# GpSimd scales the next stage's rows, and the first layer's row loads are tied to the current projection product

## The chip, the cores and the metric

The kernel runs on one core of a Trainium2 chip. The metric is the device time of one execution in microseconds (us). Three timed runs of the kernel before took 2790.7, 2800.73 and 2800.74 us; the median is 2800.73 us. Each engine works through its own list of instructions in order. Engines wait for one another, and for transfers, by semaphores. The engines are named TensorE (PE, with PEld for its weight loads), VectorE (DVE), ScalarE (ACT), GpSimd (POOL) and SyncE (SP), which here only issues DMAs.

## The reference

Two layers work on a sequence of 2048 rows of 1024 numbers, in float32. Each layer normalises every row, projects it, runs two groups of four heads, projects back and adds the result to its input. A last normalisation closes the trunk.

```python
def hybrid_layer(x, norm_w, w_in, ...):
    h = rmsnorm(x, norm_w)
    proj = jnp.einsum('bsd,de->bse', h, w_in)
    mq, mk, mv, mi, mf, mz, aq, ak, av, az = jnp.split(proj, idx, axis=-1)
    ...   # convolution and SiLU on mq, mk; mLSTM over chunks; per-head norm, skip, gate -> ym
    ...   # rotary on aq, ak; softmax1 - lam*softmax2 over earlier chunks; per-head norm, gate -> ya
    y = jnp.einsum('bse,ed->bsd', jnp.concatenate([ym, ya], -1), w_out)
    return x + y

def rmsnorm(x, w):
    y = x * lax.rsqrt(jnp.mean(x * x, axis=-1, keepdims=True) + EPS)
    return y * w
```

The change concerns the first line, `rmsnorm(x, norm_w)`: the sum of squares of each row, and the product of the row with its scale factor.

## The kernel before

**Stages and units.** The 2048 rows are cut into four blocks of 512 (T). A stage is one block in one layer, so there are eight stages; stage s of layer 0 is followed by stage s + 1 on the next block. A stage has four units, one per head of both groups. In a unit TensorE makes the head's projection products (512 rows, the eight 128-column pieces of the input), its attention scores, the products of the weights with the values, and the mLSTM products. The two output projections of a stage are worked off in the stage's last unit and the next stage's second.

**Precision.** Most products are made of split numbers: an operand is stored as a rounded high half and the rest as a low half, and three products are added. A weight tile is therefore loaded (`wr`, L191, SyncE), rounded (`wh`, L193, ScalarE) and subtracted (`wl`, L195, GpSimd). Each of the three has three buffers.

**Preparing a stage's input.** This is what the change touches. `prep_x` (L223) finds the scale factors of the next stage's rows. In layer 1 it reads sums of squares that the output projection of layer 0 left behind. In layer 0, for stages 1 to 3, `row_scale` (L199) loads each of the four 128-row pieces in two halves of 256 KB (L204, eight loads into the four buffers of tile x), ScalarE squares and sums each half (L205), VectorE adds the two sums and makes the mean (L210, L211), GpSimd raises it to the power -1/2 (L212). This call stands at the start of unit 2 (L1080). `prep_t` (L249) then fetches the rows again in four quarters of 256 columns (L258, two loads each, the same four buffers), scales them in place (L272, four instructions of 128x256 per quarter, 16 per stage), transposes them on TensorE (L109), and splits the result into `hth` (L278, ScalarE) and `htl` (L280, VectorE). The first two quarters are fetched early, ahead of the last unit's output projection; a later quarter is fetched when the buffers of an earlier one are free. Stage 0 has its own way (`prep_first`, L231) and isn't touched. So L272 runs 7 x 16 = 112 times.

**The value products of a stage's first head** are evicted by ScalarE (L344, L346) and VectorE (L345), and with them the gate values (gt, L348, VectorE). Only then is their accumulator free for TensorE.

**Rotary work of the next head.** `post_b` (L440) makes the rotated q and k: two VectorE products, four on GpSimd (L448 to L451), then two tiles ab, whose high halves ScalarE rounds (L456) and whose low halves GpSimd subtracts (L457). Sixteen small DMAs (L460, L461) copy pieces of ab into the q and kc tiles from which TensorE makes the next unit's scores.

**What sets the order.** A planner gives every piece of work a time and a stream. TensorE's instructions are tied together: each follows the last of its stream, and a projection product (stream P) also follows all side work (scores A, weights times values V, mLSTM M) that is planned 15 us or more ahead of it. The other engines are ordered by the scheduler of the language, which takes an instruction when its operands and buffers are free in its own model. `after(r, name)` (L87) adds an order without a wait: the scheduler places r behind the named instruction. `last_pe["P"]` is the name of the latest projection product at that point of the program.

Of the kernel before, what the change touches and what calls it, by code (L numbers as in the profile page):

```python
# [16 lines left out]
ALU = mybir.AluOpType  # L17
AX = mybir.AxisListType

P = 128  # L20
S = 2048
D = 1024
T = 512
# [29 lines left out]
def trunk_kernel(ctx, tc, x, w_ch, w_v0, w_v, w_o, nw, cw, cb, gb, mnw, msk, anw, lam,  # L53
                 fnw, rope, out, n_layers=NL, n_t=NT):
    nc = tc.nc
    V, A, G, PE, SY = nc.vector, nc.scalar, nc.gpsimd, nc.tensor, nc.sync
# [11 lines left out]
    def st(shape, tag, dt=F32, name=None):  # L68
        return sb.tile(shape, dt, tag=tag, name=name or tag, bufs=BUFS[tag])

    def sm(cols, name):
        return sb.tile([P, cols], F32, tag="s_" + name, name=name, bufs={"mx": 2, "zc": 2, "nm": 2, "s12": 4}.get(name, 1))

    def pst(tag, shape):
        return psm.tile(shape, F32, tag=tag, name=tag, bufs=PB[tag])

    def f32(ap):
        return ap.bitcast(F32)
# [3 lines left out]
    last_pe = {}  # L82
# [4 lines left out]
    def after(r, name):  # L87
        tc.add_manual_dep(r.ins, name, nosync, reason="TensorE order")
# [19 lines left out]
    def tr(o, i, n=P):  # L108
        pin(PE.transpose(o, i, ident[:n, :n]))  # L109
# [75 lines left out]
    def xin(l, t):  # L185
        return x[t * T:(t + 1) * T, :] if l == 0 else xo[l - 1][t]
# [12 lines left out]
    def row_scale(src, tb, tag):  # L199

        sq = sm(2, "xsq")
        for hf in range(2):
            xt = st([P, T], tag)
            SY.dma_start(xt, src[tb * P:(tb + 1) * P, hf * T:(hf + 1) * T])  # L204
            A.activation(xt, xt, AF.Square, accum_out=sq[:, hf:hf + 1])  # L205
        return row_rms(sq)

    def row_rms(sq):
        rs = sb.tile([P, 1], F32, tag="s_xrs", name="xrs", bufs=8)
        V.tensor_tensor(rs, sq[:, 0:1], sq[:, 1:2], op=ALU.add)  # L210
        V.tensor_scalar(out=rs, in0=rs, scalar1=1.0 / D, scalar2=EPS, op0=ALU.mult, op1=ALU.add)  # L211
        G.tensor_tensor(rs, rs, mhalf[:, 0:1], op=ALU.pow)  # L212
        return rs[:, 0:1]
# [9 lines left out]
    def prep_x(l, t):  # L223
        if l > 0:
            return row_scales(sqs[l - 1, t])
        return [row_scale(xin(l, t), tb, "x") for tb in range(4)]
# [22 lines left out]
    def prep_t(l, t, rs, H, rows=None):  # L249
        pr = par[l]  # L250
        src = xin(l, t)
        qs = {}

        def fetch(q):

            qs[q] = [st([P, 2, 256], "x") for _ in range(2)]
            for i, xt in enumerate(qs[q]):
                SY.dma_start(xt, src[2 * i * P:2 * (i + 1) * P, q * 256:(q + 1) * 256].rearrange("(b p) c -> p b c", p=P))  # L258

        def task(dc):  # L260
            def f():
                if dc == 0:
                    H["rope"] = sb.tile([P, 2, T], F32, tag="rope", name="rope", bufs=1)
                    SY.dma_start(H["rope"], rope[t])
                q, j = divmod(dc, 2)
                if rows:
                    xs = [r_[dc // 4][:, (dc % 4) * P:(dc % 4 + 1) * P] for r_ in rows]
                else:
                    if j == 0:
                        for tb in range(4):  # L270
                            xb = qs[q][tb // 2][:, tb % 2]
                            V.tensor_scalar(out=xb, in0=xb, scalar1=rs()[tb], scalar2=None, op0=ALU.mult)  # L272
                    xs = [qs[q][tb // 2][:, tb % 2, j * P:(j + 1) * P] for tb in range(4)]
                ps = pst("mm", [P, T])
                for tb in range(4):
                    tr(ps[:, tb * P:(tb + 1) * P], xs[tb])
                h = st([P, T], "hth", F32R)
                A.activation(h, ps, AF.Copy, scale=pr["nw"][:, dc:dc + 1])  # L278
                lo = st([P, T], "htl", F32R)
                r_ = V.scalar_tensor_tensor(out=lo, in0=ps, scalar=pr["nw"][:, dc:dc + 1], in1=f32(h),  # L280
                                            op0=ALU.mult, op1=ALU.subtract)
                if rows and dc == 7:
                    first["r"] = r_.ins.name
                H["hh"].append(h)
                H["hl"].append(lo)
                if not rows and j == 1 and q < 2:
                    fetch(q + 2)
            return f

        H["fetch"] = lambda: (fetch(0), fetch(1))  # L290
        return [(0.44, task(dc)) for dc in range(8)]
# [966 lines left out]
```

## Time and profile before

| | |
|---|---|
| median of three runs | 2800.73 us |
| profiled execution | 2792.97 us |
| its span, first to last instruction | 2791.3 us |
| TensorE busy | 2656.9 us, 95% |
| VectorE busy | 1796.1 us, 64% |
| ScalarE busy | 1688.5 us, 60% |
| GpSimd busy | 1439.6 us, 52% |
| mean granted TensorE clock | 0.988 |

Busy is the time in which an engine works on an instruction. Idle time of TensorE is what can be won or lost directly; idle time of the others matters only where TensorE waits for them. A row of waits gives the engine and line that waited, the one that released it, the total, the number and the longest. A row of the timeline gives the start and the length in us, the engine, the line, the operation, the tiles, how many instructions were merged, and in brackets how long the engine stood idle before it and what ended that. The mean granted clock is below 1 where TensorE ran at 1.2 GHz instead of 2.4.

### The profile page before, as it was taken

The page shows a single profiled execution, that of the slowest core. Times are in us where ns is not written, and L with a number is a line of the kernel's source. Part 1 is how long each engine was busy: PE and PEld are TensorE (multiplying, and loading weights), DVE is VectorE, ACT ScalarE, POOL GpSimd, SP SyncE. Part 2 cuts the span into 40 slices and gives each one's busy share as a digit, 9 for nine tenths or more (in the row PEclk, how much of TensorE's full clock was granted, in tenths as well). Part 3 has the DMA queues.
Part 4 walks back from the last instruction along what each step waited for, and adds up shares of the span by engine and source line. Part 5 has one row for each costly group of instructions (what it writes and reads, how often), then busy time and mean ns, then how long its engine had stood idle before and what let it go on. Part 6 is the DMA issues. An engine that isn't in the chain of part 4 may idle for free. (4 is left out here: it accounts for less than half of the span.)

```text
span 2791.3 us, 49265 instructions
## 1 busy us (share of the span) xinstructions
PE 2656.9 (95%) x16692; PEld 2359.0 (85%) x16692; DVE 1796.1 (64%) x4746; ACT 1688.5 (60%) x4541; POOL 1439.6 (52%) x1182
## 2 busy tenths in 40 slices
PE   7999999999999999999999999999999999999997
PEld 6898898888888888888889888978888888887887
DVE  5546565665757767567755465666667676676776
ACT  5655566666656656565556555656566665665665
POOL 5564656545455354344446656555554554445425
PEclk9999999999999999999999999999999999999999
DMA  6645555464644644344556465654557445455333
GB/s 211 173 133 159 178 163 157 135 194 140 191 141 124 189 129 140 117 115 130 162 144 182 142 184 156 196 182 136 177 145 223 145 133 178 118 181 149 100 104 121
DMA packets 249788, 431.01 MB, mean 154 GB/s; under 512 B 30400, under 2 KB 106688, under 8 KB 249536
## 3 DMA queue, kind: packets, MB, share of 16 engines
q1 hardware_dynamic: 249536, 427.87, 51.4%
q8 instruction: 132, 2.16, 0.3%
q14 instruction: 120, 0.98, 0.1%
HBM read 314.38 MB, written 63.05 MB: 135 GB/s over the span
## 5 line engine op out<-in xcount | busy, mean ns | idle before, releaser
L195 POOL TENSOR_TENSOR wl<-wr,wh 128x512 fp32r<-128x512 f32 (+1 forms) x684 | 910.5, 1337 | 1030.7 <-PE mm L106 418.4
L193 ACT ACTIVATE wh<-wr 128x512 fp32r<-128x512 f32 (+1 forms) x684 | 429.1, 629 | 402.6 <-PE mm L106 185.4
L106 PE MATMUL mm<-hth,wh 128*128 128x512 f32 x1536 | 620.1, 404 | 0.0
L106 PE MATMUL mm<-htl,wh 128*128 128x512 f32 x1536 | 611.0, 398 | 0.0
L740 DVE TENSOR_SCALAR_CACHE_REDUCE p<-sc 128x512 f32<-128x512 f32 (+3 forms) x640 | 384.2, 605 | 140.0 <-PE sc L106 113.6
L684 ACT ACTIVATE p<-p,nm 128x512 f32<-128x512 f32 (+3 forms) x640 | 413.9, 649 | 95.8 <-DVE nm L680 87.8
L106 PE MATMUL mm<-hth,wl 128*128 128x512 f32 x1536 | 438.0, 399 | 0.0
L106 PEld LDWEIGHTS mm<-hth,wh 128*128 128x128 f32 x1536 | 291.2, 190 | 59.3 <-ACT vaug L346 0.9
L106 PEld LDWEIGHTS mm<-htl,wh 128*128 128x128 f32 x1536 | 291.3, 190 | 57.2
L106 PEld LDWEIGHTS mm<-hth,wl 128*128 128x128 f32 x1536 | 283.8, 189 | 60.2
L807 DVE TENSOR_TENSOR atl<-tpa,ath 128x512 fp32r<-128x512 f32 x288 | 197.2, 685 | 144.0 <-ACT ath L806 143.0
L704 DVE SCALAR_TENSOR_TENSOR p<-p,s 128x512 f32<-128x512 f32 (+2 forms) x320 | 280.7, 888 | 1.7
L106 PE MATMUL mm<-wh,hth 128*128 128x256 f32 (+1 forms) x1024 | 264.9, 289 | 10.9 <-DVE gt L348 10.5
L106 PE MATMUL mm<-wh,htl 128*128 128x256 f32 (+1 forms) x1024 | 262.0, 286 | 0.0
L806 ACT ACTIVATE ath<-tpa 128x512 fp32r<-128x512 f32 x288 | 170.2, 591 | 148.1 <-PE tpa L109 142.5
L106 PE MATMUL sc<-kp,q 128*128 128x512 f32 x768 | 244.7, 406 | 9.3 <-DVE p L740 9.2
L106 PEld LDWEIGHTS mm<-wh,hth 128*128 128x128 f32 x1024 | 196.1, 191 | 15.8 <-issue 11.5
L106 PEld LDWEIGHTS mm<-wh,htl 128*128 128x128 f32 x1024 | 196.4, 192 | 2.9
L109 PE MATMUL tpa<-ident,p 128*128 128x128 f32 x1088 | 184.4, 274 | 13.3 <-DVE tpa L799 7.4
L409 DVE SCALAR_TENSOR_TENSOR cacc<-mm,cw,cacc 128x511 f32<-128x511 f32 (+2 forms) x192 | 143.1, 745 | 75.6 <-ACT cacc L405 69.2
L106 PE MATMUL pv<-ath,vp 128*128 128x256 f32 x768 | 178.2, 286 | 3.8 <-ACT ath L806 3.8
L106 PE MATMUL mm<-wl,hth 128*128 128x256 f32 (+1 forms) x1024 | 164.6, 289 | 0.0
(212 smaller groups left out, 5626.2 us busy)
## 6 DMA issues: line engine op xcount, KB each, us to landing
wr<-in_w_ch_dram SPq DMA_DIRECT2D x384, 256.0 KB, 2.7
wr<-in_w_o_dram SPq DMA_DIRECT2D x140, 256.0 KB, 2.9
q<-ab SPq DMA_DIRECT2D x256, 128.0 KB, 2.4
vp<-vd SPq DMA_DIRECT2D x48, 512.0 KB, 4.3
wr<-in_w_v_dram SPq DMA_DIRECT2D x96, 256.0 KB, 3.7
kp<-kd SPq DMA_DIRECT2D x48, 512.0 KB, 4.0
wr<-in_w_v_dram SPq DMA_DIRECT2D x64, 264.0 KB, 3.2
kc<-ab SPq DMA_DIRECT2D x256, 64.0 KB, 2.0
```

What stands on the lines that cost most here:

```text
L106: pin(PE.matmul(o, l, r, start=start, stop=stop, skip_group_check=True))
L109: pin(PE.transpose(o, i, ident[:n, :n]))
L193: A.activation(wh[:, :n], wr[:, :n], AF.Copy)
L195: G.tensor_tensor(wl[:, :n], wr[:, :n], f32(wh[:, :n]), op=ALU.subtract)
L409: V.scalar_tensor_tensor(out=acc[:, d:], in0=ps[:, 0:T - d], scalar=w(j), in1=acc[:, d:], op0=ALU.mult, op1=ALU.add)
L684: A.activation(pp[:, :w], pp[:, :w], AF.Exp, bias=nm[:, m:m + 1], accum_out=zc[:, m, kt:kt + 1])
L704: d_ = V.scalar_tensor_tensor(out=pc[0][kt][:, :w], in0=pc[1][kt][:, :w], scalar=cq["s"][:, 0:1], in1=pc[0][kt][:, :w], op0=ALU.mult, op1= ...
L740: ev = V.tensor_scalar(out=pp[:, :w], in0=ps[:, :w], scalar1=0.125, scalar2=None, op0=ALU.mult, op1=ALU.max, accum_out=c["mx"][:, m, kt:kt ...
L806: A.activation(ah, p2, AF.Copy)
L807: lo_ = V.tensor_tensor(al, p2, f32(ah), op=ALU.subtract)
```

## The change

Two lines differ. The scaling L272 is issued on GpSimd instead of VectorE, and each of the row loads L204 is placed behind the latest projection product. Nothing else in the source differs.

```diff
@@ -201,7 +201,7 @@
         sq = sm(2, "xsq")
         for hf in range(2):
             xt = st([P, T], tag)
-            SY.dma_start(xt, src[tb * P:(tb + 1) * P, hf * T:(hf + 1) * T])
+            after(SY.dma_start(xt, src[tb * P:(tb + 1) * P, hf * T:(hf + 1) * T]), last_pe["P"])
             A.activation(xt, xt, AF.Square, accum_out=sq[:, hf:hf + 1])
         return row_rms(sq)
@@ -269,7 +269,7 @@
                     if j == 0:
                         for tb in range(4):
                             xb = qs[q][tb // 2][:, tb % 2]
-                            V.tensor_scalar(out=xb, in0=xb, scalar1=rs()[tb], scalar2=None, op0=ALU.mult)
+                            G.tensor_scalar(out=xb, in0=xb, scalar1=rs()[tb], scalar2=None, op0=ALU.mult)
                     xs = [qs[q][tb // 2][:, tb % 2, j * P:(j + 1) * P] for tb in range(4)]
```

The scheduler's order changes with it. The first place is VectorE's list at the start of the program, at the evictions of the first head's value products (vc, gt); rows with a minus are gone.

```order
 L345 TENSOR_TENSOR vc<-mm,vc 128x128 x2
-L210 TENSOR_TENSOR xrs<-xsq 128x1
-L272 TENSOR_SCALAR x<-x,xrs 128x256 x2
-L211 TENSOR_SCALAR xrs<-xrs 128x1
 L348 TENSOR_TENSOR gt<-mm,gb_275 128x8 x2
-L272 TENSOR_SCALAR x<-x,xrs 128x256 x6
 L345 TENSOR_TENSOR vc<-mm,vc 128x128 x2
```

Sums and scalings of stage 1, which the scheduler had pulled to the start of stage 0 because the x buffers were free, no longer stand around the gate tile.

The second place is GpSimd's list in stage 0, at the rotary work of the third head (ab_1947 and ab_1958 are its two ab tiles). Before, from the last of the four rotary products to the second ab:

```order
L451 TENSOR_TENSOR t2_1936<-t2_1936,ra_1859 128x512
L457 TENSOR_TENSOR ab_1947<-t3_1939,ab_1947 128x512
L195 TENSOR_TENSOR wl_2207<-wr_2203,wh_2205 128x512
L331 MEMSET vaug_2348 128x4
L457 TENSOR_TENSOR ab_1958<-t2_1936,ab_1958 128x512
```

And now, in the same place:

```order
L451 TENSOR_TENSOR t2_1936<-t2_1936,ra_1859 128x512
L212 TENSOR_TENSOR xrs_2000<-xrs_2000,mhalf_71 128x1
L195 TENSOR_TENSOR wl_2207<-wr_2203,wh_2205 128x512
L272 TENSOR_SCALAR x_2979<-x_2979,xrs_1978 128x256
L457 TENSOR_TENSOR ab_1947<-t3_1939,ab_1947 128x512
L272 TENSOR_SCALAR x_2979<-x_2979,xrs_1989 128x256
L212 TENSOR_TENSOR xrs_2011<-xrs_2011,mhalf_71 128x1
L331 MEMSET vaug_2348 128x4
L272 TENSOR_SCALAR x_2983<-x_2983,xrs_1978 128x256
L272 TENSOR_SCALAR x_2983<-x_2983,xrs_1989 128x256
L272 TENSOR_SCALAR x_2980<-x_2980,xrs_2000 128x256
L457 TENSOR_TENSOR ab_1958<-t2_1936,ab_1958 128x512
```

Five scalings and two powers stand in these rows in front of the second ab; two more powers stand just above, among L448 to L450. In the same place of stage 1 it is eight scalings, in that of stage 2 six.

The third place is SyncE's list of DMAs at the same point. Before:

```order
L191 DMA wr_2203<-in_w_ch_dram 128x512
L191 DMA wr_2241<-in_w_ch_dram 128x512
L461 DMA kc_1944<-ab_1947 32x512 x2
L191 DMA wr_2264<-in_w_ch_dram 128x512
L563 DMA bc_2910<-bw0_0_712 128x2x512
```

And now, from the last of the first four row loads on:

```order
L204 DMA x_1986<-in_x_dram 128x512
L191 DMA wr_2203<-in_w_ch_dram 128x512
L204 DMA x_1994<-in_x_dram 128x512
L204 DMA x_1997<-in_x_dram 128x512
L191 DMA wr_2241<-in_w_ch_dram 128x512
L204 DMA x_2005<-in_x_dram 128x512
L204 DMA x_2008<-in_x_dram 128x512
L258 DMA x_2979<-in_x_dram 128x2x256
L258 DMA x_2980<-in_x_dram 128x2x256
L258 DMA x_2983<-in_x_dram 128x2x256
L191 DMA wr_2264<-in_w_ch_dram 128x512
L461 DMA kc_1944<-ab_1947 32x512 x2
```

The eight row loads of stage 1 and three of its first four fetches stood in the first 30 us of the program; now they stand between weight loads, ahead of the copies into kc and q.

## Rows read from the trace of the kernel before

**Rows 1.** The page's head and part 1: busy us, share, instructions.

```profile
span 2791.3 us, 49265 instructions
...
PE 2656.9 (95%) x16692; PEld 2359.0 (85%) x16692; DVE 1796.1 (64%) x4746; ACT 1688.5 (60%) x4541; POOL 1439.6 (52%) x1182
```

**Rows 2.** Waits of TensorE: who waited for whom, total us, times, longest.

```profile
PE pv L106 <- DVE atl L807: 24.0, 33, 3.0
...
PE mm L106 <- DVE gt L348: 10.5, 5, 2.7
...
PE mm L106 <- POOL wl L195: 0.6, 2, 0.4
```

**Rows 3.** L272 by shape (busy us, mean ns), and what it waited for.

```profile
L272 DVE TENSOR_SCALAR x<-x,rs 128x256 f32<-128x256 f32 x64 | 30.7, 520 | 27.9 <-DMA x<-xo 23.0 <-ACT hs L601 4.7
...
L272 DVE TENSOR_SCALAR x<-x,xrs 128x256 f32<-128x256 f32 x48 | 22.3, 508 | 11.8 <-DMA x<-in_x_dram 11.3 <-POOL xrs L212 0.4
...
  DMA x<-xo: 23.0, 17
  DMA x<-in_x_dram: 11.3, 8
```

**Rows 4.** Stretches: length, busy per engine (instructions), granted clock, DMA share, GB/s.

```profile
260.00:270.00 10.00, 7.05 (x48) 6.23 (x47) 7.90 (x24) 4.73 (x12) 2.54 (x2) 0.84 0.49 159
...
1640.00:1650.00 10.00, 7.05 (x45) 6.29 (x44) 8.27 (x26) 4.65 (x12) 2.54 (x2) 0.79 0.48 153
...
sum 150.00, PE 118.90 PEld 105.75 DVE 123.49 ACT 85.64 POOL 46.45; mean PE 7.93 PEld 7.05 DVE 8.23 ACT 5.71 POOL 3.10
```

**Rows 5.** The same fifteen stretches, L272 alone: the sum.

```profile
sum 150.00, DVE 28.71; mean DVE 1.91
```

**Rows 6.** Timeline at the start, VectorE and TensorE.

```profile
30.36 0.48 DVE L345 TENSOR_TENSOR vc<-mm,vc 128x128 fp32r<-128x128 f32 x2
...
31.74 0.62 DVE L272 TENSOR_SCALAR x<-x,xrs 128x256 f32<-128x256 f32 x2
...
32.33 0.23 DVE L348 TENSOR_TENSOR gt<-mm,gb 128x8 f32<-128x8 f32 x2
...
32.64 0.36 PE L106 MATMUL mm<-wh,hth 128*128 128x264 f32 x1 [2.73 <-DVE gt L348]
```

**Rows 7.** Timeline at a boundary of layer 0: VectorE, GpSimd, TensorE.

```profile
439.70 2.92 DVE L272 TENSOR_SCALAR x<-x,xrs 128x256 f32<-128x256 f32 x3 [0.43 <-POOL xrs L212]
...
443.67 0.67 DVE L807 TENSOR_TENSOR atl<-tpa,ath 128x512 fp32r<-128x512 f32 x1
...
439.63 2.57 POOL L195 TENSOR_TENSOR wl<-wr,wh 128x512 fp32r<-128x512 f32 x2
...
444.40 0.58 PE L106 MATMUL pv<-atl,vp 128*128 128x256 f32 x1 [2.95 <-DVE atl L807]
```

**Rows 8.** GpSimd's instructions by shape: a one-input one, and the power.

```profile
L573 POOL TENSOR_SCALAR_AFFINE_SELECT bc<-bc 128x512 f32<-128x512 f32 x32 | 20.6, 643 | 33.2 <-ACT bc L572 28.3 <-DVE sc L738 3.6 <-PE sc L106 1.3
...
L212 POOL TENSOR_TENSOR xrs<-xrs,mhalf 128x1 f32<-128x1 f32 x16 | 8.8, 552 | 26.2 <-DVE xrs L211 24.8 <-DVE gt L348 1.4
```

**Rows 9.** Timeline of TensorE: the first product with one weight tile and with the next.

```profile
38.08 0.39 PE L106 MATMUL mm<-hth,wh 128*128 128x512 f32 x1
...
40.84 0.39 PE L106 MATMUL mm<-hth,wh 128*128 128x512 f32 x1
```

**Rows 10.** Rotary work of stage 0's third head, to the first score; a median landing.

```profile
175.49 1.30 POOL L457 TENSOR_TENSOR ab<-t,ab 128x512 fp32r<-128x512 f32 x1
...
178.66 1.14 SPq L460 DMA_DIRECT2D q<-ab  x2
...
182.38 0.59 SPq L461 DMA_DIRECT2D kc<-ab  x1
...
kc<-ab SPq DMA_DIRECT2D x256, 64.0 KB, 2.0
...
186.03 0.28 PE L106 MATMUL sc<-kc,q 128*128 128x256 f32 x1
```

## The prediction, made before the result was known

> **What bounds the kernel now.** I read the page's busy times first, then TensorE's waits, then the rows of the changed line, then stretches of ten microseconds around it. TensorE is busy 2656.9 of 2791.3 us [rows 1], so it sets the time, and 134.4 us is all that it ever stands idle. Its waits are short and many: the longest totals are on VectorE's low halves of the attention weights and on the gate tile (10.5 us in 5 waits), and GpSimd's low halves of the projection weights cost it 0.6 us in all [rows 2]. So GpSimd (52% busy) holds TensorE up nowhere much, and VectorE (64%) does at certain places.
>
> The scaling (L272) runs 112 times on VectorE, at a mean of 520 and 508 ns, and VectorE stood idle in front of it for 34.3 us in 25 waits for the row loads [rows 3], with everything behind it in VectorE's order held too. Fifteen stretches of 10 us hold most scalings that have a TensorE stall close by. There TensorE is idle 150 - 118.9 = 31.1 us [rows 4]; outside them it is idle 103.3 us in 2641 us, or 5.9 us per 150. The excess is 25.2 us. Two of the stretches also show a granted clock of 0.84 and 0.79 [rows 4]: part of them ran at the lower level (1.2 GHz) behind the stall, worth another 1.6 + 2.1 = 3.7 us. So 29 us is the most that those stretches can give back.
>
> **The change, part by part.** I count against the profiled execution, 2792.97 us (span 2791.3 and 1.7 us around it). The three timed runs are 2790.7, 2800.73 and 2800.74, so this execution lies near the low one, 8 us under the median.
>
> *Start.* Before, the first squares' row loads stand in the first 30 us, and VectorE does sums, scale factors and eight scalings between the first value product's eviction and the gate tile. TensorE waits 2.73 us for that tile; VectorE could have started it at 30.36 + 0.48 = 30.84 and started it at 32.33 [rows 6]. All of this leaves the start. Gain 1.5 us (none if the eviction by ScalarE, in the same order, were late as well; 2.7 at most).
>
> *VectorE relieved.* In the fifteen stretches VectorE is busy 123.5 us [rows 4], 28.7 us of it scaling [rows 5]. Without that it is busy 94.8 of 150, 63%, its share of the whole kernel [rows 1], and the 34.3 us of waiting for loads goes to another queue. The plainest place: three scalings take 2.92 us beside two GpSimd subtractions, the low half that TensorE waits for starts at 443.67, and TensorE has then stood 2.95 us [rows 7]. Taking that share at its word, the whole 29 us would go. But these stretches are stage boundaries, where VectorE also evicts the output product and makes the next stage's low halves, and those stay. I take 60%, 17 us; ends 0 and 29.
>
> In rows 7 a scaling beside GpSimd takes about 1 us, where two undisturbed ones take 0.62 us together [rows 6]. The Trainium skill's page "SBUF — State Buffer", section "Who interferes with whom", says why: VectorE's fast two-port form and GpSimd share a port pair, and the later of the two is blocked for a whole instruction. By that rule the move removes locked time from both; by the same rule GpSimd's new reads can block VectorE's two-input instructions. That makes no term of its own here: the sum by it is the same one.
>
> *GpSimd's new work.* The trace shows no such operation on GpSimd. The nearest rows: one input of 512 elements takes 643 ns, so 256 elements take at least half, 0.32 us [rows 8]; two inputs of 512 take 2.57 / 2 = 1.29 us [rows 7], which I take as the upper end. The nearer row is the first (one input, the same 128 partitions, a fixed part within it); I take 0.5 us, so 112 x 0.5 = 56 us on an engine that is idle for 1352 us. What it hides behind is GpSimd's lead: the low halves have three buffers, TensorE uses one up in 40.84 - 38.08 = 2.76 us [rows 9], so two buffers cover 5.5 us. A stage's first eight scalings take 8 x 0.5 = 4.0 us, and a wait for rows of 34.3 / 25 = 1.4 us on average makes 5.4 us: just covered. The second eight come as two sets of four, 2.0 us each. Cost 2 us, for places where the lead is not full (0 to 34, see the last rival).
>
> The Trainium skill's "GPSIMD Engine Reference", section "Engine selection", calls one-input work on GpSimd about line rate and two-input work about twice as slow as VectorE's. Two rows here are in that direction (643 against 1290 ns for 512). By the page a scaling's streaming would be an estimated 256 / 1.2 GHz = 0.21 us and the fixed part on top; that is the third rival's side.
>
> *Row loads in the middle of the stage.* For the three later stages of the first layer, eight row loads, eight squares, four powers and the first eight scalings now stand where the next head's rotary work is on GpSimd and where its sixteen small copies into q and kc are on SyncE. In front of the second ab stand, newly, four powers at 0.552 us [rows 8] and five, eight and six scalings (stages 1, 2, 3): 4.7, 6.2 and 5.2 us. Of slack there is: the second ab ends at 175.49 + 1.30 = 176.79, the first copy that needs it is issued at 178.66, which is 1.9 us; the last copy is issued at 182.38 and lands a median 2.0 us later, at 184.4, and the first score with that q runs at 186.03, which is 1.6 us [rows 10]. Together 3.5 us, so TensorE would stand 1.2 + 2.7 + 1.7 = 5.6 us. The scalings also wait for their rows in front of the ab subtraction: 1.4 us each time, 4.2 us. One of the stalls may bring the lower clock, 1.6 us as in the stretch at 260 us. Cost 11 us. Ends: nothing, if the copies' queue has more room than this one unit shows; 26 us, if the rows are 4.5 us late each time (23.0 / 17 is 1.4 on average, and what is queued behind the scaling on GpSimd is the ab subtraction, behind it SyncE's copies, behind them the score) and every stall brings the lower clock.
>
> SyncE's own queue: eleven row loads more stand ahead of the copies, and the row loads past the fourth wait for a square to free their buffer. The weight loads among them have the same lead of three buffers; I cost that at nothing beyond the 1.4 us.
>
> **Sum.** -1.5 - 17 + 2 + 11 = -5.5 us on 2793.0: 2787.5 us, so 2788.
>
> **Rivals.**
> (a) *The scaling's lateness only changes its engine.* Rows come late by 4.5 us in front of the ab subtraction: 3 x 3.1 = 9.3 us more and two more stretches at the lower clock, 3.2 us, so -5.5 + 12.5 = +7: 2800 us, no change. For it: 34.3 us of such waits on VectorE [rows 3], and the loads now start later. Against it: the average wait is 1.4 us.
> (b) *More is given back.* A scaling takes 0.32 us, so in front of the second ab stand 3.8, 4.8 and 4.1 us against 3.5 of slack (2 us in all), no lead is lost, and all of the 29 us goes: -1.5 - 29 + 2 = -28.5, and 2766 with some wait for rows. For it: VectorE's share without the scalings is the kernel's mean. Against it: the other boundary work.
> (c) *Slower: GpSimd becomes late for TensorE.* The place is each stage's first eight scalings, the price 8p + 1.4 - 5.5 us at seven boundaries, and 19p + 6.6 - 10.5 + 4.2 + 1.6 us for the rotary work, for a scaling of p us. At p = 0.6 that is 5 + 13 us and eats up the gain of 18.5; from p = 0.9 on (22 + 19) it is 22 us longer, 2815 us; at 1.29, the two-input price, it would be 44 + 26 - 18.5 = +52, about 2845. For it: ordinary arithmetic on GpSimd is slow in this trace, a power of one element per partition takes 0.55 us [rows 8]. Against it: the row with one input.
>
> **How the numbers follow.** 0.5% of the median is 14 us, about what a measurement of this kernel can tell from no change: faster is under 2786.7, slower over 2814.7. The forecast has 0.40, with its own range 2774 to 2798 (its 60% may be 40 or 90), half of it on the faster side; (a) 0.22, nearly all of it within the bound; (b) 0.20, faster; (c) 0.18, of which 0.15 lies over 2814.7. Faster 0.21 + 0.20 = 0.41; slower 0.15 and 0.04 of (a), 0.19; the rest 0.40. The range 2758 to 2822 takes in (a), most of (b) and the lower half of (c).
>
> **What would show it.** Right: L272 on GpSimd at about 0.5 us; TensorE's wait for the gate tile at about 32 us shrunk to 1.2; in VectorE's waits no rows from a load before L272; TensorE's idle time at the stage boundaries down by half or more; new waits of one to three microseconds of TensorE in front of a score in the third head of the first three stages. Wrong: waits of TensorE for wl or for the transposed rows (price over 0.6 us); idle time of GpSimd in front of L272 well over 1.4 us each; boundary stalls of the same total that now name another instruction of VectorE, which would say that the scaling was not what held them.

## The result, and the profile after

| | before | after |
|---|---|---|
| median, first comparison | 2799.62 us (5 runs) | 2779.97 us (5 runs) |
| ratio | | 0.9947, 95% interval 0.9931 to 0.9962 |
| median, second chip session | 2791.86 us (17 runs) | 2775.90 us (6 runs) |
| ratio | | 0.9935, interval 0.9913 to 0.9957 |
| profiled execution, span | 2791.3 us | 2776.2 us |

The ratios are those on record with their intervals; the quotients of the medians are 0.9930 and 0.9943. Predicted were 2788 us, 5.5 us less than the profiled execution; it became 15 us less, and 16 to 20 us by the medians. Executions of one and the same kernel spread over some 20 us (before: 2779.5 to 2802.4 in 35 runs), so one trace against another says little under 10 us. Below, each finding is asked of more than one trace.

The page after, against [rows 1]. TensorE is busy 7.2 us less, at least in part since less of its work ran at the lower clock (granted clock 0.990, before 0.988), and GpSimd 102 us more.

```profile
span 2776.2 us, 49297 instructions
PE 2649.7 (95%) x16692; PEld 2353.4 (85%) x16692; DVE 1759.2 (63%) x4634; ACT 1685.4 (61%) x4541; POOL 1541.8 (56%) x1294
```

The changed line on GpSimd, against [rows 3]: count, then shortest, median and longest duration in ns; below it what GpSimd's idle time in front of it ended on, in us and times.

```profile
L272 POOL TENSOR_SCALAR x<-x,rs x64: 917/924/1465, 1118.5 to 2309.8; 128x256 f32<-128x256 f32 x64
L272 POOL TENSOR_SCALAR x<-x,xrs x48: 913/924/1890, 175.1 to 946.7; 128x256 f32<-128x256 f32 x48
  DMA x<-xo: 45.7, 11
  DMA x<-in_x_dram: 28.1, 6
```

The median is 0.924 us where I took 0.5, and GpSimd waits 73.8 us in 17 waits for rows, 4.3 us each, where I took 1.4. Yet TensorE's waits, against [rows 2], name GpSimd's low halves of the weights for 2.2 us only:

```profile
PE pv L106 <- DVE atl L807: 17.8, 29, 1.6
PE ml L109 <- ACT hs L622: 14.9, 5, 5.6
PE mm L106 <- DVE xr L929: 10.0, 8, 2.9
PE mm L106 <- DVE gt L348: 8.6, 7, 2.9
PE tpa L109 <- POOL vaug L331: 3.1, 1, 3.1
PE mm L106 <- POOL wl L195: 2.2, 3, 1.1
```

The start, against [rows 6]: VectorE goes from the value product's eviction straight to the gate tile, and TensorE waits 1.34 us for it (before 2.73).

```profile
30.32 0.49 DVE L345 TENSOR_TENSOR vc<-mm,vc 128x128 fp32r<-128x128 f32 x2 [3.42 <-ACT vc L344]
30.95 0.37 DVE L348 TENSOR_TENSOR gt<-mm,gb 128x8 f32<-128x8 f32 x2
31.27 0.36 PE L106 MATMUL mm<-wh,hth 128*128 128x264 f32 x1 [1.34 <-DVE gt L348]
```

To see where the time went, I cut both spans at the same evictions of the convolution (one per head). Four stretches differ most: heads 2 and 3 of stage 0, the second head of stage 1, the second head of stage 2, and the first stage of the second layer with the boundary behind it. A row gives the stretch, its length, the busy times (TensorE's first) and, third from the end, TensorE's granted clock. Before:

```profile
108.40:227.00 118.60, 116.38 (x674) 101.41 (x673) 60.99 (x180) 69.75 (x191) 72.18 (x61) 0.97 0.48 142
383.10:480.20 97.10, 91.79 (x606) 83.47 (x605) 55.00 (x153) 61.72 (x185) 54.67 (x49) 0.98 0.60 179
713.30:820.90 107.60, 101.35 (x646) 89.85 (x647) 69.22 (x181) 70.12 (x204) 52.87 (x45) 0.97 0.54 164
1401.30:1703.40 302.10, 290.60 (x1836) 260.08 (x1835) 163.84 (x444) 169.09 (x463) 174.72 (x142) 0.98 0.55 163
```

After, between the same evictions:

```profile
106.90:232.80 125.90, 118.78 (x681) 102.26 (x681) 59.73 (x189) 73.89 (x208) 82.63 (x73) 0.97 0.54 159
384.80:475.90 91.10, 90.35 (x608) 82.49 (x608) 50.47 (x144) 63.55 (x186) 53.87 (x47) 1.00 0.63 186
711.60:812.20 100.60, 98.17 (x660) 89.52 (x659) 67.53 (x167) 69.91 (x202) 52.62 (x46) 1.00 0.58 177
1395.20:1691.40 296.20, 288.01 (x1836) 257.83 (x1835) 156.10 (x429) 167.43 (x462) 187.63 (x158) 0.99 0.55 166
```

One is longer, three are shorter by 6 to 7 us each, and in the two second heads the clock is back at 1.00. For all kernels the same cuts give this table of TensorE's loss: its idle time, plus half of the time at the lower clock, in us, one trace each. At the top stand the scaling's engine (V VectorE, G GpSimd, A ScalarE) and whether the row loads are free or tied.

| stretch | before V free | e3 V free | e1 G free | e11 G, tie on stage 1 | e2 V tied | after G tied | e5, its 2nd trace | e6 V/G tied | e12 V/G tied | e8 A tied |
|---|---|---|---|---|---|---|---|---|---|---|
| start | 17.1 | 16.9 | **27.3** | 16.0 | 16.2 | 18.4 | 15.9 | 17.2 | 15.3 | 16.0 |
| stage 0, heads 2 and 3 | 5.6 | 5.6 | 7.5 | 11.9 | 8.3 | **10.6** | **12.3** | 8.2 | 7.7 | 7.2 |
| stage 1, second head | **7.0** | **3.7** | 2.6 | 1.6 | 0.0 | 0.8 | 0.0 | 0.6 | 0.5 | 0.0 |
| stage 2, second head | **9.6** | **13.6** | **10.6** | **11.6** | 2.4 | 2.4 | 2.4 | 2.9 | 2.4 | 4.3 |
| layer 1, first stage | **16.7** | **15.8** | 12.3 | 8.3 | **16.6** | 9.9 | 10.4 | 7.9 | 12.3 | 6.0 |
| whole span | 167.8 | 159.2 | 165.5 | 164.6 | 161.2 | 154.3 | 161.5 | 154.2 | 156.3 | 149.0 |

The records of the clock begin some 15 to 25 us into each trace, so the first row says less than the others: 1.7 us of the 18.4 after are a low clock at 20.7 us, where the records of before have not begun. The five rows do not add up to the whole. From before to after they fall by 13.9 us and the whole by 13.5; but in e2 they fall by 12.5 and the whole by 6.6, in the second trace of the change by 15.0 and the whole by 6.3. So other heads lose some of the gain again in these two, and no cause was found for that.

### The profile page after: what moved, and what is told of

It is laid out like the page before. It is cut to its first block, busy times and chain, and to the rows that moved or that the text cites. A ratio compares the mean times of both kernels' runs of the same rounds, so it can differ in the third digit from the quotient of the medians.

```text
span 2776.2 us, 49297 instructions
## 1 busy us (share of the span) xinstructions
PE 2649.7 (95%) x16692; PEld 2353.4 (85%) x16692; DVE 1759.2 (63%) x4634; ACT 1685.4 (61%) x4541; POOL 1541.8 (56%) x1294
## 5 line engine op out<-in xcount | busy, mean ns | idle before, releaser
L195 POOL TENSOR_TENSOR wl<-wr,wh 128x512 fp32r<-128x512 f32 (+1 forms) x684 | 907.0, 1332 | 894.4 <-PE mm L106 388.6
L704 DVE SCALAR_TENSOR_TENSOR p<-p,s 128x512 f32<-128x512 f32 (+3 forms) x320 | 287.4, 910 | 1.8
```

The lines of the kernel that those rows point to most:

```text
L195: G.tensor_tensor(wl[:, :n], wr[:, :n], f32(wh[:, :n]), op=ALU.subtract)
L704: d_ = V.scalar_tensor_tensor(out=pc[0][kt][:, :w], in0=pc[1][kt][:, :w], scalar=cq["s"][:, 0:1], in1=pc[0][kt][:, :w], op0=ALU.mult, op1= ...
```

## The experiments

**e1, GpSimd without the tie.**

```diff
-            after(SY.dma_start(xt, src[...]), last_pe["P"])
+            SY.dma_start(xt, src[...])
```

> Only the scaling moves to GpSimd; the row loads stay untied. Theory 1 (the 20 us come from VectorE losing 112 scalings and the waits in front of them): 2777 to 2784 us, ratio to before 0.992 to 0.995; TensorE's wait for the gate tile of the first head short as well, since no scaling stands in front of it on VectorE; VectorE about 1759 us busy. Theory 2 (the tie is what gains, by the start and by where the row loads stand): 2793 to 2801 us. Theory 3 (neither part does it; any new order of the scheduler moves the time by several us): anywhere between 2785 and 2800, and the two parts do not add up to the whole.

Measured: 2791.46 us, ratio 1.0011 (0.9990 to 1.0031). Theory 1, which I had formed on seeing the result, falls: no gain of the move alone shows. In its trace TensorE still waits 2.84 us for the gate tile, though no scaling is left on VectorE. VectorE's rows there say why: it stands idle 0.82 us for ScalarE's square, then does sum and mean, then the gate tile.

```profile
30.38 0.48 DVE L345 TENSOR_TENSOR vc<-mm,vc 128x128 fp32r<-128x128 f32 x2
31.67 0.16 DVE L210 TENSOR_TENSOR xrs<-xsq 128x1 f32<-128x1 f32 x1 [0.82 <-ACT x L205]
31.86 0.15 DVE L211 TENSOR_SCALAR xrs<-xrs 128x1 f32<-128x1 f32 x1
31.94 0.24 DVE L348 TENSOR_TENSOR gt<-mm,gb 128x8 f32<-128x8 f32 x2
```

And GpSimd's eight scalings stand among the first low halves of the weights: TensorE waits 0.48 us for one of these and then 2.76 us for the gates, whose chain of small steps on VectorE runs beside GpSimd's subtractions and scalings.

```profile
37.79 2.73 POOL L272 TENSOR_SCALAR x<-x,xrs 128x256 f32<-128x256 f32 x3
40.56 1.27 DVE L482 SCALAR_TENSOR_TENSOR ge<-gt 128x16 f32<-128x16 f32 x1
41.81 1.19 PE L106 MATMUL mm<-hth,wl 128*128 128x512 f32 x4 [0.48 <-POOL wl L195]
47.59 0.28 PE L109 MATMUL ml<-ident,glf 128*16 128x128 f32 x1 [2.76 <-DVE glf L498]
```

In the change the same L482 takes 0.18 us; here it ran beside one of the subtractions (L195, 40.48 to 41.76 us). The start loses 27.3 us here, 17.1 before and 15.3 to 18.4 in the tied traces.

**e2, the tie with VectorE scaling.**

```diff
-                            G.tensor_scalar(out=xb, in0=xb, scalar1=rs()[tb], ...)
+                            V.tensor_scalar(out=xb, in0=xb, scalar1=rs()[tb], ...)
```

> Only the tie; the scaling stays on VectorE. Theory 1: 2796 to 2801 us, ratio 0.998 to 1.001; the wait for the gate tile falls from 2.73 to about 1.3 us and that is all of the gain; VectorE waits about 34 us for row loads in front of its scalings, as before. Theory 2: 2780 to 2786 us. Theory 3: off from 2799.6 by 5 us or more in either direction, without a wait in the trace that the tie explains.

Measured: 2784.04 us, ratio 0.9984 (0.9967 to 1.0002). Alone, the tie gives a quarter to a third of the whole by these centres; its interval reaches from nothing to a half and more. TensorE's wait for the gate tile falls as in the change:

```profile
31.02 0.36 PE L106 MATMUL mm<-wh,hth 128*128 128x264 f32 x1 [1.35 <-DVE gt L348]
```

The table shows that the tie gives more than the start, in the second heads of stages 1 and 2; that is taken up below (e11).

**e3 and e4, another order with the same work.**

```diff
-MD = 9.0
+MD = 9.1
```

> The kernel before with one planner number changed that has nothing to do with scalings or row loads (the lead of the mLSTM work, MD, 9.1 for 9.0): the same work on the same engines, in an order that differs on every engine. Theory 1: within 4 us of before, 2795.6 to 2803.6. Theory 3 (a new order alone is worth several us): off by 5 to 15 us in either direction.

> The changed kernel with the same planner number at 9.1. Theory 1: the gain over before stays, 2776 to 2785 us. Theory 3: the gain depends on the order and shrinks or grows by 5 us or more: under 2775 or over 2785.

Measured: 0.9982 (0.9968 to 0.9995) for before, 2784.23 us; 0.9959 (0.9942 to 0.9976) for after, 2776.98 us. A planner number without meaning for this change is worth about 5 us, which is the size of the tie's own effect: no gain of the tie alone can be told from that of a new order. Between the two replanned kernels the change is worth 7 us by medians (2784.23 to 2776.98), where it is worth 16 to 20 with the number at 9.0. So a gain stays, but some 9 of the 16 us may belong to the order of one planner setting and not to the two edits.

**e5, the change again.**

> The changed kernel, unaltered, beside some thirty runs of the kernel before on one chip, since single executions of one kernel were seen to spread over 20 us. Theory 4 (the two edits pay only together: with the tie the scalings stand where GpSimd has room, without it they stand in the start): ratio 0.993 to 0.997, about 14 us under before. Theory 5 (the gain is no larger than that of any new order; moving one planner number gave 0.9982): ratio 0.997 to 1.0.

Measured: 0.9935 (0.9913 to 0.9957). Theory 4 holds for this planner setting: the change is clear of either edit alone (1.0011 and 0.9984).

**e6 and e12, GpSimd for part of the scalings.** The tie stays; e6 scales on GpSimd in the second layer (64), e12 in its last three stages (48).

```diff
-G.tensor_scalar(out=xb, ...)
+(G if l > 0 else V).tensor_scalar(out=xb, ...)              # e6
+(G if l > 0 and t > 0 else V).tensor_scalar(out=xb, ...)    # e12
```

> The tie stays; GpSimd scales only for the second layer (64 scalings), VectorE for the first (48). The prediction's step on row loads in the middle of the stage put 11 us of loss on the scalings in front of the second ab of the first layer: if that loss is in the changed kernel, this one is 4 to 11 us faster than it. If GpSimd's place in the rotary work costs nothing and each scaling taken off VectorE pays alike, it loses 48 of 112 parts of the step from the tie alone to the whole change (about 8 us): 3 to 4 us slower than the change, ratio to before about 0.996.

> The tie stays; GpSimd scales only for the last three stages of the second layer (48 of the 112 scalings), VectorE all others. Summed over idle time and lower clock, the traces so far say that moving the scaling gives back some 10 us, all of it at the stage boundaries of the second layer, and costs in the first layer what it gives there. If so, 48 scalings give the whole step from the tie alone (0.9984) to the change (0.9935 and 0.9947): ratio 0.991 to 0.995. If every scaling taken off VectorE pays alike: 0.9984 - 48/112 x 0.0044 = 0.9965, from 0.9955 to 0.9975.

Measured: e6 0.9936 (0.9917 to 0.9954), e12 0.9967 (0.9950 to 0.9983). e6 equals the whole change, so 48 scalings more on GpSimd in the first layer bring nothing, and neither of the two expectations for it came. From that I expected e12 to give all of it as well; it gave about half, what a plain count of scalings would say (0.9965). How the gain divides over the stages stays open: the intervals of e6 and e12 touch.

**e7, GpSimd scales twice.**

```diff
+                            G.tensor_scalar(out=xb, in0=xb, scalar1=1.0, scalar2=None, op0=ALU.mult)
```

> Each scaling on GpSimd is followed by a second GpSimd multiplication of the same tile by 1.0: about 103 us more of GpSimd work at 0.92 us each, nothing else. By the prediction's cover (two buffers of wl, 5.5 us, against eight scalings in a row) a stage's start would be late by 16 x 0.92 + 1.4 - 5.5 = 10.6 us at seven boundaries and the rotary work by more: 2860 us or longer, and TensorE's waits for wl in tens of us. If GpSimd has more cover than that (it stands idle for 1234 us of the changed kernel): within 10 us of the change, 2772 to 2790, with TensorE's waits for wl under 10 us.

Measured: 2799.53 us, ratio 1.0024 (1.0010 to 1.0038); by medians 24 us more than the change. The second multiplication takes a median 0.849 us. Neither expectation holds as written: not 80 us, but more than 10. Nor did the edit do quite what it was meant to: the scheduler put the second multiplications later, and in the third head of stage 0 none stands in front of the second ab. What it did make is more scaling between two low halves of the weights: over 5.5 us of it in 17 places, up to 8.9 us, where the change has two such places. TensorE's waits for GpSimd in it:

```profile
PE tpa L109 <- POOL ar L844: 10.6, 8, 2.7
PE mm L106 <- POOL wl L195: 4.2, 7, 1.4
```

So it is not the low halves of the weights that run out first; GpSimd's small power for the attention norm (ar) does, 10.6 us against 3.3 after the change (and 6.3 before it). The two rows have grown by 9.3 us together; which waits make up the rest of the 24 us was not taken apart. About a quarter of added GpSimd time (24 of some 95 us) reaches the end.

**e8, ScalarE scales.**

```diff
+                            A.activation(xb, xb, AF.Copy, scale=rs()[tb])
```

> The tie stays and ScalarE does the scaling (its nearest row: 128x256 in 0.41 us, so 46 us more on an engine that is busy for 1685). If what pays is that VectorE is rid of the scalings, this is as fast as the change, ratio 0.993 to 0.997. If it is GpSimd's lower cost in that place: slower than the change by 4 us or more, since ScalarE is released late at the same boundaries (it evicts the weights and the transposes of x).

Measured: 2772.98 us, 0.9933 (0.9913 to 0.9953): as fast as the change. With the tie in place, what pays is that VectorE is rid of the scalings; which of the other two takes them does not show.

**e9, the price by itself.**

> Not the computation: no reference output, only rows of single instructions on one 128-partition float32 tile, first GpSimd alone (one input with a scale factor per partition, one input with a constant, two inputs; 64 to 512 elements), then GpSimd beside VectorE (each of the two with one input, 256 or 512 elements, or with two, 512). The scaling of 128x256 took a median 0.92 us in the changed kernel, where 0.5 was predicted. If that is the plain price of the operation: 0.90 to 0.93 us with VectorE idle too, and about 1.7 us for 512 elements. If VectorE's traffic makes it long: 0.4 to 0.6 us alone, 0.9 us beside VectorE. For the locked pair that the prediction named: VectorE's one-input instruction beside GpSimd's should be longer than 0.6 us for 512 elements, or GpSimd's longer than alone.

GpSimd alone, by form: busy, then the mean in ns.

```profile
L66 POOL TENSOR_SCALAR y512ptr<-big,one 128x512 f32<-128x512 f32 x6 | 9.4, 1571 | 0.0
L66 POOL TENSOR_SCALAR y256ptr<-big,one 128x256 f32<-128x256 f32 x6 | 5.6, 931 | 0.0
L68 POOL TENSOR_SCALAR y256imm<-big 128x256 f32<-128x256 f32 x6 | 5.1, 857 | 0.0
L70 POOL TENSOR_TENSOR y512two<-big 128x512 f32<-128x512 f32 x6 | 6.3, 1049 | 0.0
L70 POOL TENSOR_TENSOR y256two<-big 128x256 f32<-128x256 f32 x6 | 3.7, 622 | 0.0
```

Rows with two in their name multiply a tile by itself. 0.93 us is the plain price with VectorE idle: (1571 - 931) / 256 = 2.5 ns per element and 0.29 us fixed. Then both engines at once, in one execution. A name that begins with z is GpSimd's work, one with v VectorE's; the next part is VectorE's form, the last GpSimd's (ptr: one input with a factor; two: two inputs):

```profile
L66 POOL TENSOR_SCALAR ztwoptr<-gatetwoptr,one 128x256 f32<-128x256 f32 x12 | 17.2, 1432 | 1.1
L66 POOL TENSOR_SCALAR zptrptr<-gateptrptr,one 128x256 f32<-128x256 f32 x12 | 12.8, 1065 | 1.1
L66 DVE TENSOR_SCALAR vptrtwo<-gateptrtwo,one 128x512 f32<-128x512 f32 x30 | 22.7, 757 | 3.2 <-POOL gateptrtwo L89 2.2
```

**e10, the row work 15 us later.**

```diff
-                at(xc, lambda s=s: rs0.__setitem__(...))
+                at(xc + 15.0, lambda s=s: rs0.__setitem__(...))
```

> The change, with the row loads, squares and powers of the next stage planned 15 us later in the third head, behind the copies into q and kc. The prediction put 11 us on these in front of the second ab. In the changed kernel's trace unit times of stage 0 slip by 7.3 us between the second and the fourth head (8.7 in its second trace). If that slip is what the prediction meant: gone here, and 4 to 11 us faster than the change, 2765 to 2772 (ratio 0.990 to 0.992). If the row work costs the same wherever it stands (ScalarE's squares, the loads' share of the DMA engines): within 3 us of the change, ratio 0.9925 to 0.9955, with the slip at a later head.

Measured: 2777.33 us, 0.9956 (0.9940 to 0.9971), not faster than the change. The loss in heads 2 and 3 of stage 0 is 10.5 us, as after (10.6), though the second ab now starts at 174.99 us with no scaling and no power between the two: it does not hang on standing in front of the second ab. In the new place ScalarE waits in its order for the rows of a square, 1.27 us; the attention norm's small steps on ScalarE and VectorE (to L842) come behind it, and then a score:

```profile
188.30 0.63 ACT L205 ACTIVATE x<-x 128x512 f32<-128x512 f32 x1 [1.27 <-DMA x<-in_x_dram]
191.02 0.47 PE L106 MATMUL sc<-kc,q 128*128 128x256 f32 x2 [2.24 <-DVE ar L842]
```

**e11, the tie on the second stage's rows alone.**

```diff
-            after(SY.dma_start(xt, src[...]), last_pe["P"])
+            r_ = SY.dma_start(xt, src[...])
+            if first_only:                      # rows of the second stage
+                after(r_, last_pe["P"])
```

> GpSimd scales; only the row loads for the second stage are tied, those for the third and fourth stay free. Moving the scaling without the tie gained nothing (1.0011), and its trace is 6.7 us late by the first head already, where eight scalings stand among the first weights' low halves. If the start is why the two edits need each other: ratio 0.993 to 0.996. If the later stages' ties matter as much: 0.997 to 1.0.

Measured: 2785.46 us, 0.9981 (0.9963 to 0.9998). The start is short (16.0 us in the table), and by the centres some two thirds of the gain are still missing; the traces differ by 9 us in one stretch, the second head of stage 2, which loses 11.6 us (after: 2.4), as with all free rows. There the squares for stage 3 stand in the output product of stage 1, and ScalarE waits for their rows in its order. In e11 (whose lines are two higher, L207 is the square):

```profile
754.07 0.63 ACT L207 ACTIVATE x<-x 128x512 f32<-128x512 f32 x1 [4.71 <-DMA x<-in_x_dram]
757.85 0.63 ACT L207 ACTIVATE x<-x 128x512 f32<-128x512 f32 x1 [1.62 <-DMA x<-in_x_dram]
764.34 0.36 ACT L821 ACTIVATE ot<-pv 128x256 f32<-128x256 f32 x1
764.75 0.69 PE L109 MATMUL tpa<-ident,ot 128*128 128x128 f32 x2 [1.99 <-ACT ot L821]
```

Before, the same place:

```profile
754.92 0.63 ACT L205 ACTIVATE x<-x 128x512 f32<-128x512 f32 x1 [4.80 <-DMA x<-in_x_dram]
757.12 0.38 PE L106 MATMUL pv<-ath,vc 128*128 128x256 f32 x1 [0.86 <-ACT ath L806]
765.33 0.69 PE L109 MATMUL tpa<-ident,ot 128*128 128x128 f32 x2 [1.79 <-ACT ot L819]
```

## Why the prediction was right or wrong

*Start, -1.5.* Right in place and size: the wait went from 2.73 to 1.34 us. e1 corrects the reason: there the gate tile is late without any scaling on VectorE, held by the sums that wait for ScalarE's squares; the tie alone removes that (1.35 us in e2).

*GpSimd's new work, +2, at 0.5 us each.* The price was mis-sized: 0.93 us. I had bounded one input of 256 elements by half of a row whose operation (an affine select) is another one; the upper bound, two inputs of 512, held, but per element two inputs are the cheaper form (622 against 931 ns for 256). The Trainium skill's "GPSIMD Engine Reference", section "Engine selection", calls one-input work about line rate and two-input work about twice as slow as VectorE's; in these rows one input with a factor is the dearer form, also against the sum of two different tensors (724 ns for 256 in the same run), and the measurement decides. (By that rate my estimate was 0.21 us of streaming, which stands on the side of rival (b), not of the last one.) At the measured price the last rival asked for a loss of 22 us and more. It did not come: TensorE's wait for the low halves rose from 0.6 to 2.2 us. I had set eight scalings in a row against the cover; in the trace after, at most four stand between two low halves in 28 of 31 places (3.7 us), and only two places pass 5.5 us. The cover was mis-sized too: e7 has 17 places over 5.5 us, and there the wait is 4.2 us in all. How large the lead is was not measured. What does become late on GpSimd is ar, which the prediction did not name.

*Row loads in the middle of the stage, +11.* The size was near, but here a step of the mechanism failed: the loss is not that of the scalings in front of the second ab. In stage 0 the second ab starts at 181.49 us instead of 175.49 [rows 10], 6.0 us later where I had 4.7 and 1.4 for the rows. But TensorE stalls earlier in its order, on ScalarE. The rows of GpSimd, ScalarE and TensorE:

```profile
181.49 1.29 POOL L457 TENSOR_TENSOR ab<-t,ab 128x512 fp32r<-128x512 f32 x1
181.72 0.99 ACT L572 ACTIVATE bc<-bc,cols 128x128 f32<-128x128 f32 x3 [2.86 <-DMA bc<-bw]
185.31 0.37 ACT L819 ACTIVATE ot<-pv 128x256 f32<-128x256 f32 x1
185.74 0.44 PE L109 MATMUL tpa<-ident,ot 128*128 128x128 f32 x2 [2.75 <-ACT ot L819]
```

The same load on ScalarE before, and in e2, where GpSimd has no scaling:

```profile
178.62 1.28 ACT L572 ACTIVATE bc<-bc,cols 128x128 f32<-128x128 f32 x4 [1.07 <-DMA bc<-bw]
179.81 1.28 ACT L572 ACTIVATE bc<-bc,cols 128x128 f32<-128x128 f32 x4 [5.34 <-DMA bc<-bw]
```

The mLSTM's broadcast load bc is issued on SyncE behind the row loads, at 175.20 instead of 173.23 us, and lands after 6.5 us instead of 5.4; ScalarE waits for it, and what stands behind it is late. That this wait makes the loss is read from the order, and not shown by a run: in e1 ScalarE waits 3.22 us for the same load, and TensorE loses 0.7 us in that head. What the runs show is that the loss goes with the tied row loads (and the squares and powers behind them) and not with the scalings: in the third head of stage 0 alone TensorE loses 0.0 to 0.7 us in the three traces without a tied load there, and 4.0 to 5.6 in the seven with one, whichever engine scales. In its two traces the change loses 5.0 and 6.7 us more than before in heads 2 and 3 of stage 0; with the tie and another engine's scaling 2.7 (e2) and 1.6 (e8). In the third head of stage 1 it loses 3.0 and 1.3 us more, in that of stage 2 0.5 and 0.2, with no wait for q in either. That is 8 us in all. e10 speaks against the place in front of the second ab as the cause: the loss came along to the new place.

*The term that was missing.* I priced the place to which the row work went and, but for the start, not the places that it left. Free, the squares for stages 2 and 3 stood in ScalarE's order inside an output product one head earlier (at 421 and 755 us) and waited there for their rows: such waits are 11.3 us there before, 9.4 in e1, 11.1 in e11, and none with the tie. ScalarE's idle time in front of its squares in the whole span, in us and times, before and after:

```profile
  DMA x<-in_x_dram: 11.3, 5
  DMA x<-in_x_dram: 1.2, 2
```

In the second heads of stages 1 and 2 TensorE lost 13.2 to 17.3 us in the four traces with free rows there, and 2.4 to 4.3 in the six tied ones of the table. Most of it is the second place: from 755 to 780 us TensorE waits 5.2 us before, 5.3 in e1 and 6.1 in e11, and from 740 us to the end of that head 0.0 after and 0.6 in e2; behind the squares at 421 us it is one wait of some 1.1 us. Of my fifteen stretches only 770 to 780 us lies in the second place. So some 8 to 10 us of gain stood in no term; between the predicted -5.5 and the measured -15 lie 9.5. e11 against the change shows it, since only the ties of these squares' loads differ. The tie as a whole is worth less, 5.5 us by medians (e2), since it also brings the loss told above. (The first of the two stretches holds the stall of [rows 7]. It is gone in e1 and in e2 alike, so moving the scaling or moving the rows removes it, and the difference of the two cannot be given to one of them.)

*VectorE relieved, -17.* With the tie in place, taking the scalings off VectorE is the step from 0.9984 (e2) to 0.9935 or 0.9947, some 10 to 14 us, and ScalarE as the new owner does as well (e8). That is near -17 + 2 as a total, but not in the places from which I took it. Of the fifteen stretches, twelve lie in eight heads other than the two second heads and the last head of layer 1's first stage; there TensorE loses 52.1 us before, 54.7 in e2, 51.6 and 59.8 in the two traces of the change. So its idle time at the boundaries is not down by half, and where most of the step from e2 to the change comes from stays open. It shows most clearly in the first stage of the second layer, which has no tied loads: 15.8 to 16.7 us lost with VectorE scaling in three traces, 6.0 to 12.3 in the seven others. In e1, without the tie, that stage loses 12.3 us too, but the start, where the scalings meet the first weights on GpSimd, takes 10.2 us back.

Two readings of the rows were off. The view of [rows 4] has a granted clock of 0.83 at 440 and at 1130 us and of 0.93 at 1330 as well, so five stretches and not two show the lower clock, and the most that they could give back was 33 us and not 29. And the gate tile's 10.5 us are the fifth of TensorE's totals, not one of the longest.

So the number, 2788, came out 8 us over the median of 2780 by one term left out. That it came so near is in part luck: the price of a scaling and what hides it were both wrong in ways that cancelled, and the gain on VectorE is not at the places from which its size was taken. Rival (b), 2766, named the direction for a reason that is refuted (a scaling at 0.32 us); (a) did not come, and (c) begins where e7 stands.

No version tried beats the change beyond its interval; e8 (2772.98 us) and e6 (2774.25 us) are level with it. Open are how the gain of moving divides over the stages, how much of it belongs to one planner setting (e3, e4), and, with one trace per run, which part of the differences under 5 us in the table is chance.

## What to carry to other kernels

When work is moved in an in-order queue, price the place that it leaves as carefully as the one it enters, on every engine that has a part of it; here the squares on ScalarE, which no changed line names, were worth some 8 to 10 us, nearly as much as the scaling. Two edits that do little apart (1.0011 and 0.9984) can be worth 0.6% together, when one clears the place into which the other would put its work. Before a gain of that size is credited to an edit, a new order without meaning should be tried beside it: here one was worth 5 us. A price for an engine is measured on the operation itself: a row of another operation of the same shape was off by a factor of two.

## What was not expected of the hardware

- GpSimd's multiplication by a scale factor per partition costs 2.5 ns per element of a partition (0.93 us for 256, 1.57 for 512, alone); its product of a tensor with itself 1.67 ns per element ((1049 - 622) / 256).
- Beside VectorE's two-input instructions GpSimd's scaling takes 1.43 us instead of 0.93, beside its one-input ones 1.07. The other way, VectorE's one-input instruction of 512 elements takes 1.11 us beside GpSimd's two-input ones (13.31 us busy for 12 in the window) and 0.47 when GpSimd is done (8.39 for 18). So in these rows a one-input instruction of one engine is slowed by half or more when the other has two inputs; the kernel's scaling took 0.924 us at the median all the same, so most ran undisturbed.
